# FFN down projection: nine of eleven feature pairs as 2x2x2 block products with their operands prepared in the gate/up stage and kept in DRAM

## The chip, the cores and the metric

The kernel runs on one core of a Trainium2 chip. The metric is the device time of one execution in microseconds. The kernel before takes 2179.9 us (median of three runs, 2179.11 to 2181.13).

## The reference

One step of a streaming encoder layer on 1056 rows (1024 new frames of one stream and 32 frames of another), width 1024: a half-step FFN, a token mixer (stick-breaking attention and gated linear attention beside each other), a second half-step FFN and a closing norm. The FFNs are where the change is:

```python
def swiglu(h, w_gate, w_up, w_down):
    return (jax.nn.silu(h @ w_gate) * (h @ w_up)) @ w_down

x = x + 0.5 * swiglu(rmsnorm(x, g_ffn1), w1g, w1u, w1d)
...
x = x + 0.5 * swiglu(rmsnorm(x, g_ffn2), w2g, w2u, w2d)
```

`w_gate` and `w_up` are 1024 x 2816, `w_down` is 2816 x 1024, all in float32. The 2816 hidden features are 22 tiles of 128, or eleven pairs of tiles.

## The kernel before, in words

Everything is kept transposed: features on the 128 partitions, the 1056 rows along the free dimension (`x[0..7]` are eight tiles of 128 x 1056). To keep float32 accuracy every operand is split into a high and a low part in the type fp32r: ACT copies the high part, DVE subtracts to get the low part (`split_to`, L51 and L55; POOL does the subtraction at L53 in some places). A product is then three matmuls: high by high, high by low, low by high (`mm3`, L60 to L62).

**Gate and up** are already computed as 2x2x2 block products with seven products in the place of eight (`Step`, `PRODUCTS`, `ORDER`). For each of ten feature pairs there are two steps, one for gate and one for up. A step takes the products in the order 1, 6, 7, 5, 2, 4, 3; each is 24 matmuls with 264 moving columns (L334): four k-tiles, two column slices, three split terms. The sums live in four PSUM tiles `acc_a` to `acc_d` of two banks. Products 1, 7 and 5 write a, c and d; products 2, 4 and 3 add to the same tiles later in the step, so that TensorE must wait until the first contents have been read: c1 by ACT (L347), u2, u3 and the outputs by DVE (L350, L353, L374, L380, L383). POOL makes the sums of weight blocks of the next step (L305 to L318) and, in an up step, three of the four multiplications gate by up (L384). The finished hidden tiles go to DRAM through the SP queue (`hid_spill`, L386). The first pair of each FFN is computed plainly (`Opening`).

**Down** (`Down.run`) is plain: the 22 hidden tiles come back from DRAM in groups of 4, 4, 4, 4, 2, 4, are split by ACT and DVE into `h[0..3]` and `h[4..7]` by turns, and for each of eight output tiles and three chunks of 352 columns the `mm3` of the group's tiles are summed in one PSUM tile `pd`; DVE adds half of it to `x` (L507). `Down.head` loads the first group while the last up step runs. In the last group the chunks are the outer loop, so that the norm of the next stage can start on a finished chunk.

The instructions of each engine stand in one queue and run in order. Their order is not the order in which the code emits them: a scheduler moves an instruction ahead or behind others of its engine where its operands and buffers allow. DMAs are issued from the SP queue, in its order.

Of the kernel before, what the change touches and what calls it, by code (L numbers as in the profile page):

```python
# [8 lines left out]
F32 = mybir.dt.float32  # L9
# [6 lines left out]
P = 128  # L16
# [13 lines left out]
def cs(c):  # L30
    return slice(c * CW, (c + 1) * CW)
# [93 lines left out]
}  # L125
ORDER = (1, 6, 7, 5, 2, 4, 3)


# [144 lines left out]
class Step:  # L273
# [89 lines left out]
    def out(self, q, u, ps):  # L363

        S, nc = self.S, self.S.nc
        two = lambda t: t.rearrange("p (s n) -> p s n", s=2)
        slot = lambda n: S.x[4 + q][:, n * HALF : n * HALF + HALF]
        if self.gate is None:
            sg = self.sg
            sg[q] = two(slot(1))  # L370
            if u is None:
                nc.scalar.activation(sg[q], ps, AF.Silu)
            else:
                nc.vector.tensor_add(sg[q], u, ps)  # L374
                nc.scalar.activation(sg[q], sg[q], AF.Silu)
        else:
            sg = self.gate.sg[q]
            hid = slot(0)
            if u is None:
                nc.vector.tensor_mul(two(hid), sg, ps)  # L380
            else:
                t = two(S.tmp.tile([P, HALF], F32, name="tc", tag="tc"))
                nc.vector.tensor_add(t, u, ps)  # L383
                nc.gpsimd.tensor_mul(two(hid), t, sg)  # L384
# [12 lines left out]
def gate_up(S, H, op, steps, among, between, tail, xd):  # L397
# [31 lines left out]
    for t in range(N):  # L429
        for p in ORDER:  # L430
# [4 lines left out]
            if p == 7 and t < N - 1:  # L435
                steps[t + 1].split_w()
            if t == 2 and p == 3:
                for d in range(4):
                    S.nc.sync.dma_start(S.x[d], xd[d])
            if t == N - 1:  # L440
                tail(p)

# [3 lines left out]

GROUPS = [4, 4, 4, 4, 2, 4]


class Down:  # L450


    def __init__(self, S, wd):
        self.S, self.src = S, wd
        self.n = 0

    def slab(self, raw, tag, pool):
        S = self.S
        r = raw()
        S.nc.sync.dma_start(r, self.src[self.n])  # L460
        self.n += 1
        w = pool.tile([P, 2, 1024], F32R, name="whl", tag=tag)
        split_to(S, w[:, 0], w[:, 1], r)
        return w

    def head(self, p):

        S, nc = self.S, self.S.nc
        if p in (6, 7, 5, 2):
            i = (6, 7, 5, 2).index(p)  # L470
            for h in range(2):
                raw = S.raw.tile([P, 1024], F32, name="wraw", tag="wraw")[:, :HALF]
                cols = slice(h * HALF, h * HALF + HALF)
                nc.sync.dma_start(raw, S.hidden[i][:, cols])
                split_to(S, S.h[i][:, 0, cols], S.h[i][:, 1, cols], raw)
        if p in (5, 4):
            raw2 = lambda: S.raw2.tile([P, 1024], F32, name="wraw2", tag="wraw2")
            self.first = getattr(self, "first", []) + [self.slab(raw2, "w", S.wp)]

    def run(self, after):  # L480
        S, nc = self.S, self.S.nc
        raw = lambda: S.raw.tile([P, 1024], F32, name="wraw", tag="wraw")
        f0 = 0
        for gi, n in enumerate(GROUPS):
            per = KT // n
            slabs = dict(enumerate(self.first)) if gi == 0 else {}
            base = 4 * (gi % 2)

            def get(j):
                if j not in slabs:  # L490
                    slabs[j] = self.slab(raw, "wd", S.wd)
                return slabs[j]

            def load(i):
                t = S.hraw.tile([P, NR], F32, name="hraw", tag="hraw")
                nc.sync.dma_start(t, S.hidden[f0 + n + i])
                h = S.h[4 - base + i]
                split_to(S, h[:, 0], h[:, 1], t)

            def one(d, c):  # L500
                w = get(d // per)
                pd = S.ps.tile([P, CW], F32, name="pd", tag="acc")
                for i in range(n):
                    o = i * (D // n) + (d % per) * P
                    mm3(nc, pd, w, slice(o, o + P), S.h[base + i], cs(c), i == 0, i == n - 1)
                xs = S.x[d][:, cs(c)]
                nc.vector.scalar_tensor_tensor(xs, pd, 0.5, xs, op0=ALU.mult, op1=ALU.add)  # L507

            if gi == len(GROUPS) - 1:
                for c in range(NCH):  # L510
                    for d in range(KT):
                        one(d, c)
                        if c and d == 1:
                            after(c - 1)
            else:
                m = GROUPS[gi + 1]
                for d in range(KT):
                    for c in range(NCH):
                        one(d, c)
                    if d * m // KT != (d + 1) * m // KT:  # L520
                        load(d * m // KT)
            f0 += n

# [687 lines left out]
def body(tc, A):  # L1211
# [10 lines left out]
    with ExitStack() as top:  # L1222
# [32 lines left out]
        S.wp = pool("wp", 2)  # L1255
        S.hidden = A["hid"]

        def up_pools(es, between=None):
            pool = opener(es)
            S.ps = pool("psf", 4, space=PSUM)  # L1260
            parts = pool("parts")
            S.X = [parts.tile([P, 2, HALF], F32R, name=f"part{k}") for k in range(12)]
            S.tmp = pool("tmp", 2)
# [4 lines left out]
        def down_pools(es):  # L1268
            pool = opener(es)
            S.wd, S.hraw, S.tmp = pool("wd", 4), pool("hraw", 2), pool("tmpd", 2)  # L1270
            S.ps = pool("psd", 8, space=PSUM)
# [16 lines left out]
        with ExitStack() as es:  # L1288
            up_pools(es)
            H = Halves(S, gains[:, 0], (1, 2, 3))  # L1290
# [36 lines left out]
            nc.vector.tensor_copy(S.maskb, consts[:, 2])  # L1327
        with ExitStack() as es:
            down_pools(es)
            for d in range(4, KT):  # L1330
                nc.sync.dma_start(S.x[d], A["x"][d])

# [6 lines left out]
            lr = gla_lowrank(S, A, G)  # L1339
            down.run(mix_norm)  # L1340
            q0, k0 = gla_qk(S, A, 0)
# [114 lines left out]
        with ExitStack() as es:  # L1456
# [46 lines left out]

            up_pools(es, outs)
            op.load(2)
# [17 lines left out]
            gate_up(S, H, op, steps, lambda j, n: [], between, down.head, xs)  # L1523
        with ExitStack() as es:
            down_pools(es)
            for d in range(4, KT):
                nc.sync.dma_start(S.x[d], xs[d])

# [9 lines left out]

            down.run(final)
            final(NCH - 1)  # L1540
# [20 lines left out]
def layouts(i):  # L1561
# [4 lines left out]
    def down(w):  # L1566
        out, f = [], 0
        for m in GROUPS:
            out.append(w[f * P : (f + m) * P].reshape(m, P, m, D // m).transpose(2, 1, 0, 3).reshape(m, P, D))
            f += m  # L1570
        return c(np.concatenate(out))

# [55 lines left out]
```

## Time and profile before

| what | value |
|---|---|
| time, median of three runs | 2179.9 us |
| the profiled execution: time, span | 2184.58 us, 2182.5 us |
| TensorE (PE) busy | 2110.6 us, 97% of the span, 15252 matmuls |
| VectorE (DVE) busy | 1241.2 us, 57% |
| ScalarE (ACT) busy | 809.8 us, 37% |
| GpSimd (POOL) busy | 468.9 us, 21% |
| DMA moved | 183.86 MB |
| down stage of the first FFN | from 492.7 to about 743 us |
| down stage of the second FFN | from about 1915 us to the end |

PE's busy time hides little: matmuls overlap and their ends are modelled, so that the distance between the starts of matmuls that follow each other is the time that one costs. An engine that is 57% busy over the span can be the bound in a stage of its own.

### The profile page before, as it was taken

How to read it: one execution, taken by the hardware profiler on the slowest of the kernel's cores; microseconds unless marked ns; L12 is line 12 of the kernel's file. 1: busy time of each engine (PE TensorE's matmuls, PEld its weight loads, DVE VectorE, ACT ScalarE, POOL GpSimd, SP SyncE). 2: the span in 40 equal slices, each digit the busy share in tenths (PEclk: the TensorE clock that was granted, in tenths of full speed). 3: DMA queues.
4: the chain of work that ended last, by engine and by line, in shares of the span. 5: the costliest groups of instructions: out<-in, count | busy, mean ns of one | idle time of the engine just before them, and what ended most of it. 6: DMA issues, size and time to landing. Idle time of an engine off the chain costs nothing.

```text
span 2182.5 us, 36732 instructions
## 1 busy us (share of the span) xinstructions
PE 2110.6 (97%) x15252; PEld 2042.2 (94%) x15252; DVE 1241.2 (57%) x1946; ACT 809.8 (37%) x1374; POOL 468.9 (21%) x385
## 2 busy tenths in 40 slices
PE   7999999999999989999999988899999999999998
PEld 6899999999999978888898987899999999999997
DVE  6844444455435766286766687687444444454456
ACT  6522322332112443335555565364223223321115
POOL 0133333320000221122122312101343343200000
PEclk9999999999999999999999999999999999999999
DMA  4222222226322300102203042232222222253212
GB/s 171 89 79 79 78 79 79 79 92 200 108 69 80 108 30 29 37 30 66 76 22 98 27 131 70 77 120 98 70 89 78 70 89 78 77 194 116 79 50 80
DMA packets 73351, 183.86 MB, mean 84 GB/s; under 512 B 8320, under 2 KB 29088, under 8 KB 73184
## 3 DMA queue, kind: packets, MB, share of 16 engines
q1 hardware_dynamic: 73184, 181.51, 25.5%
q8 instruction: 120, 1.97, 0.4%
q14 instruction: 47, 0.39, 0.1%
HBM read 131.21 MB, written 43.52 MB: 80 GB/s over the span
## 4 chain that ended last, share of the span: by engine, by line
PE 84%; DVE 10%; ACT 3%; issue 1%; DMA 1%; POOL 0%; DVEq 0%; SPq 0%; ACTq 0%; POOLq 0%
PE acc_a L334 11%; PE acc_c L334 11%; PE acc_d L334 11%; PE pd L60 7%; PE pd L62 7%; PE pd L61 7%; PE acc_b L334 5%; PE acc L242 4%; PE pj L60 3%; PE pj L61 3%; PE pj L62 3%; DVE f L1082 2%; PE st L587 2%; PE av L1107 1%; PE po L61 1%
## 5 line engine op out<-in xcount | busy, mean ns | idle before, releaser
L60 PE MATMUL pd<-h,whl 128*128 128x352 f32 x1056 | 342.6, 324 | 0.0
L62 PE MATMUL pd<-h,whl 128*128 128x352 f32 x1056 | 339.7, 322 | 0.0
L61 PE MATMUL pd<-h,whl 128*128 128x352 f32 x1056 | 339.7, 322 | 0.0
L334 PE MATMUL acc_a<-h,whl 128*128 128x264 f32 x1920 | 247.8, 285 | 2.0 <-DVE whl L55 2.0
L334 PE MATMUL acc_d<-part,S 128*128 128x264 f32 x1920 | 246.8, 284 | 0.0
L334 PEld LDWEIGHTS acc_a<-h,whl 128*128 128x128 f32 x1920 | 240.2, 189 | 2.2 <-DVE whl L55 2.2
L507 DVE SCALAR_TENSOR_TENSOR x<-pd,x 128x352 f32<-128x352 f32 x288 | 147.4, 521 | 162.9 <-PE pd L62 161.9
L334 PEld LDWEIGHTS acc_d<-part,S 128*128 128x128 f32 x1920 | 238.8, 188 | 0.0
L51 ACT ACTIVATE whl<-wraw 128x1024 fp32r<-128x1024 f32 x120 | 126.7, 1056 | 275.4 <-PE pd L62 190.0
L51 ACT ACTIVATE S<-s 128x512 fp32r<-128x512 f32 x160 | 101.3, 634 | 336.1 <-PE acc_d L334 155.4
L60 PE MATMUL pj<-h,whl 128*128 128x352 f32 x576 | 205.8, 357 | 0.0
L61 PEld LDWEIGHTS pd<-h,whl 128*128 128x128 f32 x1056 | 199.2, 189 | 0.4
L60 PEld LDWEIGHTS pd<-h,whl 128*128 128x128 f32 x1056 | 198.1, 188 | 0.4
L62 PEld LDWEIGHTS pd<-h,whl 128*128 128x128 f32 x1056 | 198.5, 188 | 0.0
L55 DVE TENSOR_TENSOR whl<-wraw,whl 128x1024 fp32r<-128x1024 f32 x92 | 137.2, 1492 | 100.0 <-ACT whl L51 100.0
L61 PE MATMUL pj<-h,whl 128*128 128x352 f32 x576 | 192.8, 335 | 0.0
L62 PE MATMUL pj<-h,whl 128*128 128x352 f32 x576 | 192.5, 334 | 0.0
L53 POOL TENSOR_TENSOR whl<-wraw,whl 128x1024 fp32r<-128x1024 f32 x28 | 70.6, 2522 | 371.0 <-ACT whl L51 370.9
L384 POOL TENSOR_TENSOR x<-tc,x 128x528 f32<-128x528 f32 x60 | 104.4, 1740 | 119.8 <-DVE tc L383 113.5
L334 PE MATMUL acc_b<-h,S 128*128 128x264 f32 x960 | 124.6, 285 | 1.5 <-ACT h L51 1.2
L334 PE MATMUL acc_c<-part,S 128*128 128x264 f32 x960 | 124.4, 285 | 1.1 <-DVE hid L254 1.1
L334 PE MATMUL acc_c<-h,A 128*128 128x264 f32 x960 | 123.6, 285 | 0.0
(285 smaller groups left out, 3813.5 us busy)
## 6 DMA issues: line engine op xcount, KB each, us to landing
hid_spill<-x SPq DMA_DIRECT2D x80, 264.0 KB, 2.1
hraw<-hid_spill SPq DMA_DIRECT2D x36, 528.0 KB, 4.6
wraw<-win SPq DMA_DIRECT2D x24, 512.0 KB, 3.3
wraw<-w1g SPq DMA_DIRECT2D x22, 512.0 KB, 3.7
wraw<-w1u SPq DMA_DIRECT2D x22, 512.0 KB, 3.3
wraw<-w1d SPq DMA_DIRECT2D x22, 512.0 KB, 3.8
wraw<-w2g SPq DMA_DIRECT2D x22, 512.0 KB, 3.5
wraw<-w2u SPq DMA_DIRECT2D x22, 512.0 KB, 3.3
```

Of the source, the lines that this page charges most:

```text
L51: nc.scalar.activation(hi, src, AF.Copy)
L53: nc.gpsimd.tensor_sub(lo, src, hi.bitcast(F32))
L55: nc.vector.tensor_sub(lo, src, hi.bitcast(F32))
L60: nc.tensor.matmul(out, w[:, 0, wsl], a[:, 0, asl], start=first, stop=False)
L61: nc.tensor.matmul(out, w[:, 0, wsl], a[:, 1, asl], start=False, stop=False)
L62: nc.tensor.matmul(out, w[:, 1, wsl], a[:, 0, asl], start=False, stop=last)
L242: nc.tensor.matmul(out, self.w[i](k, a), quarter(S, k, b, j), start=k == 0 and n == 0, stop=k == KT - 1 and n == 2)
L334: nc.tensor.matmul(t[:, s, :SW], w[:, a, ks], m(k, b, s), start=fresh and k == 0 and n == 0, stop=k == 3 and n == 2, skip_group_check=not ...
L384: nc.gpsimd.tensor_mul(two(hid), t, sg)
L507: nc.vector.scalar_tensor_tensor(xs, pd, 0.5, xs, op0=ALU.mult, op1=ALU.add)
L587: nc.tensor.matmul(st[:n, groups * b : groups * b + groups], sq[:, b * P : b * P + n], ones[:, :: P // groups], start=True, stop=True)
L1082: nc.vector.tensor_tensor_scan(fr, fr, fr, 1.0, op0=ALU.mult, op1=ALU.bypass)
```

## The change

Pairs 1 to 9 of each FFN (hidden tiles 2 to 19) take part in block products in the down projection too; pair 0 and pair 10 (tiles 0, 1, 20, 21) stay plain and come last.

In the gate/up stage the up step no longer stores hidden tiles for pairs 1 to 9. It keeps the seven moving operands of the pair: the blocks B11, B21, B22 and the differences T1 to T4, each split into high and low (ACT copy, DVE subtract) in one of `x[0..3]` by turns, and sends each (528 KB) to DRAM. B12 itself is not kept. The four differences are made by DVE when the last hidden block is there:

```diff
-            f, h = 2 * self.i + q // 2, q % 2
-            nc.sync.dma_start(S.hidden[f][:, h * HALF : h * HALF + HALF], hid)
+            if self.i == FT // 2 - 1:
+                f, h = 2 + q // 2, q % 2
+                nc.sync.dma_start(S.hidden[f][:, h * HALF : h * HALF + HALF], hid)
+            elif q != 1:
+                self.keep({0: "B11", 3: "B22", 2: "B21"}[q], hid)
+            else:
+                b11, b12, b21, b22 = (S.x[4 + n][:, :HALF] for n in range(4))
+                for name, o, x, y in (("T1", b11, b12, b11), ("T3", b12, b22, b12), ("T2", b22, b22, b11), ("T4", b21, b21, b22)):
+                    nc.vector.tensor_sub(o, x, y)
+                    self.keep(name, o)
+
+    def keep(self, name, src):
+        S = self.S
+        S.n_kept = getattr(S, "n_kept", 0) + 1
+        t = S.x[S.n_kept % 4].bitcast(F32R).rearrange("p (a n) -> p a n", a=2)
+        split_to(S, t[:, 0], t[:, 1], src)
+        S.nc.sync.dma_start(S.parts[self.i - 1, PARTS.index(name)], t.bitcast(F32))
```

The down stage is 20 steps: five groups of pairs, (1, 2), (3, 4), (5, 6), (7, 8) and (9), and in each group four steps, one for each pair of output tiles. A product of a group of two pairs is 12 matmuls of 264 columns, of the single pair 6. A step's weights are four blocks of the pair's weight tiles; POOL makes S1 to S4 of them, ACT and DVE split all seven:

```diff
+PAIRS = [(1, 2), (3, 4), (5, 6), (7, 8), (9,)]
+PLAIN = (0, 1, 20, 21)
...
+class DownStep:
...
+        nc.gpsimd.tensor_add(s1, a[3], a[2])
+        nc.gpsimd.tensor_sub(s2, s1, a[0])
+        nc.gpsimd.tensor_sub(s3, a[0], a[3])
+        nc.gpsimd.tensor_sub(s4, a[1], s2)
...
+        split_to(S, wa[:, 0, : 2 * w], wa[:, 1, : 2 * w], raw[:, : 2 * w])
+        split_to(S, ws[:, 0, : 2 * w], ws[:, 1, : 2 * w], s12)
+        split_to(S, wb[:, 0, :w], wb[:, 1, :w], a[2])
+        split_to(S, ws[:, 0, 2 * w : 4 * w], ws[:, 1, 2 * w : 4 * w], s34)
...
+        half = lambda out, ps, y: nc.vector.scalar_tensor_tensor(out, ps, 0.5, y, op0=ALU.mult, op1=ALU.add)
...
+            if p == 1:
+                c1 = new("s1")
+                nc.scalar.activation(c1, ps, AF.Copy, scale=0.5)
+            elif p == 6:
+                u2 = new("u2", bufs=1)
+                half(u2, ps, c1)
+            elif p == 7:
+                u3 = new("u3", bufs=1)
+                half(u3, ps, u2)
+                nc.gpsimd.tensor_add(x[1][1], x[1][1], u3)
+            elif p == 5:
+                half(x[1][1], ps, x[1][1])
+                nc.gpsimd.tensor_add(x[1][0], x[1][0], u2)
+            elif p == 2:
+                half(x[0][0], ps, x[0][0])
+                nc.gpsimd.tensor_add(x[0][1], x[0][1], u2)
+            elif p == 4:
+                half(x[1][0], ps, x[1][0])
+            else:
+                half(x[0][1], ps, x[0][1])
```

`w` is 256 for a group of two pairs and 128 for the single pair; s12 and s34 have one buffer each, `ws` (tag "w", called whl in the rows below) two. The parts of the next group are loaded from DRAM while a group runs, into the half of `h` and of the twelve tiles `X` that the group does not use. During the last four steps the four plain tiles are loaded and split (`plain_tile`), and four slabs of weights with them (`plain_slab`); `Down.plain` is then the last group of the kernel before. The weights of the down projection are laid out anew on the host.

What this does to the queues, at three places. **DVE in the down stage before**: between the additions to x (L507) stand only the splits of the next group's hidden tiles and slabs.

```order
L507 SCALAR_TENSOR_TENSOR x<-pd,x 128x352 x8
L55 TENSOR_TENSOR whl<-wraw,whl 128x1024
L507 SCALAR_TENSOR_TENSOR x<-pd,x 128x352 x5
L55 TENSOR_TENSOR h_84<-hraw,h_84 128x1056
L507 SCALAR_TENSOR_TENSOR x<-pd,x 128x352
L55 TENSOR_TENSOR h_85<-hraw,h_85 128x1056
```

DVE in a step of the down stage now (the 14th of the 20; u_7083 and u_7115 are its u2 and u3, S_7213, A_7214 and whl are the weights of the step two further on):

```order
L505 SCALAR_TENSOR_TENSOR u_7083<-pd_b,s_7065 128x528
L505 SCALAR_TENSOR_TENSOR u_7115<-pd_c,u_7083 128x528
L505 SCALAR_TENSOR_TENSOR x<-pd_d,x 128x528
L505 SCALAR_TENSOR_TENSOR x<-pd_a,x 128x528
L55 TENSOR_TENSOR S_7213<-wraw_7067,S_7213 128x512
L505 SCALAR_TENSOR_TENSOR x<-pd_c,x 128x528
L55 TENSOR_TENSOR A_7214<-wraw_7067,A_7214 128x256
L505 SCALAR_TENSOR_TENSOR x<-pd_d,x 128x528
L55 TENSOR_TENSOR whl<-s_7207,whl 128x512
L55 TENSOR_TENSOR whl<-s_7208,whl 128x512
```

The two splits that read the POOL sums s_7207 and s_7208 have moved to the end of the step, behind the last addition to x.

**POOL in the down stage**: before, three memsets are all that stands there between the last multiplications of the up step (L384) and the splits of the next stage (L53).

```order
L384 TENSOR_TENSOR x<-tc,x 128x528 x2
L573 MEMSET nv 128x9 x2
L1125 MEMSET fs 32x2
L384 TENSOR_TENSOR x<-tc,x 128x528
L53 TENSOR_TENSOR whl<-wraw,whl 128x1024 x2
```

Now (s_7085 are the sums for the 15th step, u_6961 and u_6993 are u2 and u3 of the 13th, s_7207 the sums for the 16th, u_7083 and u_7115 u2 and u3 of the 14th; L533 and L536 add u2 to two quarters of x, L530 adds u3 to the quarter that product 5 completes):

```order
L484 TENSOR_TENSOR s_7085<-wraw_6945 128x256
L485 TENSOR_TENSOR s_7085<-s_7085,wraw_6945 128x256
L486 TENSOR_TENSOR s_7086<-wraw_6945 128x256
L487 TENSOR_TENSOR s_7086<-wraw_6945,s_7085 128x256
L533 TENSOR_TENSOR x<-x,u_6961 128x528
L536 TENSOR_TENSOR x<-x,u_6961 128x528
L530 TENSOR_TENSOR x<-x,u_6993 128x528
L484 TENSOR_TENSOR s_7207<-wraw_7067 128x256
L485 TENSOR_TENSOR s_7207<-s_7207,wraw_7067 128x256
L486 TENSOR_TENSOR s_7208<-wraw_7067 128x256
L487 TENSOR_TENSOR s_7208<-wraw_7067,s_7207 128x256
L533 TENSOR_TENSOR x<-x,u_7083 128x528
```

The sums for step i+2 stand in front of the three additions of step i.

**DVE at the end of an up step** in the gate/up stage. Before, u2 and u3 of the next gate step follow the last output at once:

```order
L383 TENSOR_TENSOR tc<-u_4212,acc_d 128x528
L55 TENSOR_TENSOR S_4375<-s_4373,S_4375 128x512
L350 TENSOR_TENSOR u_4434<-s_4407,acc_b 128x528
L55 TENSOR_TENSOR S_4440<-s_4438,S_4440 128x512
L353 TENSOR_TENSOR u_4468<-u_4434,acc_c 128x528
```

Now (L394 are the differences T1 to T4, the splits named x<-x their low parts):

```order
L384 TENSOR_TENSOR tc<-u_4355,acc_d 128x528
L55 TENSOR_TENSOR S_4539<-s_4537,S_4539 128x512
L394 TENSOR_TENSOR x<-x 128x528 x2
L55 TENSOR_TENSOR x<-x 128x528
L394 TENSOR_TENSOR x<-x 128x528
L55 TENSOR_TENSOR x<-x 128x528
L394 TENSOR_TENSOR x<-x 128x528
L55 TENSOR_TENSOR x<-x 128x528 x2
L351 TENSOR_TENSOR u_4598<-s_4571,acc_b 128x528
L55 TENSOR_TENSOR S_4604<-s_4602,S_4604 128x512
L354 TENSOR_TENSOR u_4632<-u_4598,acc_c 128x528
```

Eight instructions have come between the last output of the up step and u2 of the next gate step.

More of the change, by code (lines that the diff above doesn't have):

```diff
@@ L480, in run @@
[L480 to L501, printed above, removed]
+        self.slab = 0
@@ new lines, in __init__, with part, load_part @@
+        h, X = S.h, S.X
+        h0 = lambda d: h[d][:, :, :HALF]
+        h1 = lambda d: h[d][:, :, HALF:]
+        self.places = [
+            [h0(0), h0(1), h0(2), h0(3), h1(0), h1(1), h1(2), h1(3)] + X[:6],
+            X[6:] + [h0(4), h0(5), h0(6), h0(7), h1(4), h1(5), h1(6), h1(7)],
+        ]
+        self.steps = [DownStep(self, g, m) for g in range(len(PAIRS)) for m in range(4)]
+        self.raw = {}
+    def part(self, g, n, k):
+        return self.places[g % 2][2 * n + k]
+    def load_part(self, g, n):
+        for k, i in enumerate(PAIRS[g]):
+            self.S.nc.sync.dma_start(self.part(g, n, k).bitcast(F32), self.S.parts[i - 1, n])
@@ new lines, in prep, with head, strassen, between @@
+    def prep(self, i):
+        if i < len(self.steps):
+            self.steps[i].prep(self.raw.pop(i))
+    def head(self, p):
+        if p == 1:
+            self.load_step(0)
+            self.load_step(1)
+        elif p == 6:
+            for n in range(4):
+                self.load_part(0, n)
+        elif p == 7:
+            self.load_part(0, 4)
+            self.load_part(0, 5)
+            self.prep(0)
+        elif p == 5:
+            self.load_part(0, 6)
+    def strassen(self, xd):
+        S = self.S
+        last = len(PAIRS) - 1
+        for d in range(4, KT):
+            S.nc.sync.dma_start(S.x[d], xd[d])
+        for i, st in enumerate(self.steps):
+            def between(n):
+                if n == 0:
+                    self.load_step(i + 2)
+                if n == 1:
+                    self.prep(i + 1)
+                if st.g < last and n % 2 == 0 and 4 * (n // 2) + st.m < 7:
+                    self.load_part(st.g + 1, 4 * (n // 2) + st.m)
+                if st.g == last and n in (1, 4):
+                    self.plain_tile(st.m, n // 4)
+                if st.g == last and n == 6:
+                    self.plain_slab(st.m)
+            st.emit(between)
@@ L522, in run @@
-            f0 += n
+                if c and d == 1:
+                    after(c - 1)
 def run(items, filler=()):
@@ L1255, in body, with ffn_pools @@
         S.wp = pool("wp", 2)
[L1256 to L1261, printed above, removed]
+        S.hidden, S.parts = A["hid"], A["parts"]
+        def ffn_pools(es, part, inner, between=None):
+            S.ps = opener(inner)("psf", 4, space=PSUM)
+            parts = opener(part)("parts")
             S.X = [parts.tile([P, 2, HALF], F32R, name=f"part{k}") for k in range(12)]
+            pool = opener(inner)
             S.tmp = pool("tmp", 2)
@@ L1327, in body @@
             nc.vector.tensor_copy(S.maskb, consts[:, 2])
[L1328 to L1331, printed above, removed]
+            down.strassen(A["x"])
+            inner.close()
+            plain_pools(es)
             def mix_norm(c):
@@ L1339, in body @@
             lr = gla_lowrank(S, A, G)
-            down.run(mix_norm)
+            down.plain(mix_norm)
             q0, k0 = gla_qk(S, A, 0)
@@ L1523, in body @@
             gate_up(S, H, op, steps, lambda j, n: [], between, down.head, xs)
[L1524 to L1527, printed above, removed]
+            down.strassen(xs)
+            inner.close()
+            plain_pools(es)
             def final(c):
@@ L1537, in final @@
                     nc.sync.dma_start(A["y"][d][:, cs(c)], t)
-            down.run(final)
+            down.plain(final)
             final(NCH - 1)
```

147 lines of the change are left out of this document (98 added, 49 removed).

## The prediction

> **What bounds the kernel now.** I read the page first, then the chain that ended last, then the busy time of single stretches.
>
> ```profile
> span 2182.5 us, 36732 instructions
> PE 2110.6 (97%) x15252; PEld 2042.2 (94%) x15252; DVE 1241.2 (57%) x1946; ACT 809.8 (37%) x1374; POOL 468.9 (21%) x385
> ...
> 115.94 2.93 PE acc_a L334 x24
> 118.86 2.92 PE acc_c L334 x24
> ...
> 385.00:440.00 55.00, 55.00 (x455) 55.00 (x454) 23.26 (x30) 17.30 (x26) 17.80 (x13) 1.00 0.21 69
> 550.00:605.00 55.00, 55.00 (x345) 55.00 (x344) 25.32 (x39) 9.43 (x9) 0.00 (x0) 1.00 0.32 98
> ```
>
> PE is the bound. In the gate/up stretch (385 to 440) and in the plain down stretch (550 to 605) it has no gap at the full clock, and the other engines are busy for less than half of the time; POOL does nothing in the down stretch. The chain gives the price of a product of the block form: 24 matmuls of 264 columns from 115.94 to 118.86, 2.92 us, 121.8 ns each. The down stretch gives the plain form: 345 matmuls of 352 columns touch 55.00 us, so 344 intervals, 159.9 ns each. So the first question is how many matmuls go, and the second whether the other engines, which had half of their time free, can feed a stage whose products are half as long as those of gate and up.
>
> **The matmuls.** For one pair and one of four pairs of output tiles the plain form needs 2 x 2 x 3 x 3 = 36 matmuls of 352, 36 x 0.1599 = 5.76 us; the block form 7 x 2 x 3 = 42 matmuls of 264, 42 x 0.1218 = 5.12 us. That is 0.64 us less, 9 pairs x 4 x 2 FFNs = 72 times: **-46 us** if PE never waits. The Trainium skill (TensorE: Matmul & The Clock Gate, "Back-to-back issue gap") gives for streams with weight loads about 81 ns at 128 columns and 131 ns at 512; between them by a straight line, an estimate, 352 columns would cost 110 ns and 264 columns 99 ns, and the block form would be the slower one by 13 us in all. The two rows above contradict it here: the shorter matmul is 38 ns cheaper.
>
> **The queues of a down step with two pairs.** PE needs 7 x 1.46 = 10.24 us. These rows price the rest, from the groups and from the timeline:
>
> ```profile
> L507 DVE SCALAR_TENSOR_TENSOR x<-pd,x 128x352 f32<-128x352 f32 x288 | 147.4, 521 | 162.9 <-PE pd L62 161.9 <-issue 0.8
> L350 DVE TENSOR_TENSOR u<-s,acc_b 128x528 f32<-128x528 f32 x40 | 28.2, 704 | 162.7 <-PE acc_b L334 162.7
> L55 DVE TENSOR_TENSOR S<-s,S 128x512 fp32r<-128x512 f32 x160 | 111.3, 697 | 4.5 <-ACT S L51 2.8
> L55 DVE TENSOR_TENSOR wt<-tr,wt 128x256 fp32r<-128x256 f32 x16 | 6.7, 417 | 4.2 <-ACT wt L51 4.2
> L55 DVE TENSOR_TENSOR h<-wraw,h 128x528 fp32r<-128x528 f32 x16 | 11.4, 711 | 12.8 <-ACT h L51 12.7
> L305 POOL TENSOR_TENSOR s<-wraw 128x512 f32<-128x512 f32 x38 | 48.9, 1288 | 210.1 <-DVE S L55 210.1
> ...
> 443.95 0.69 DVE L55 TENSOR_TENSOR S<-s,S 128x512 fp32r<-128x512 f32 x1
> 444.01 1.84 POOL L384 TENSOR_TENSOR x<-tc,x 128x528 f32<-128x528 f32 x1 [0.91 <-DVE tc L383]
> 445.81 1.29 POOL L305 TENSOR_TENSOR s<-wraw 128x512 f32<-128x512 f32 x1
> 446.15 0.70 DVE L380 TENSOR_TENSOR x<-x,acc_a 128x528 f32<-128x528 f32 x1 [1.51 <-PE acc_a L334]
> 447.18 1.29 POOL L308 TENSOR_TENSOR s<-s,wraw 128x512 f32<-128x512 f32 x1
> 447.25 2.30 DVE L55 TENSOR_TENSOR whl<-wraw,whl 128x1024 fp32r<-128x1024 f32 x1 [0.39 <-ACT whl L51]
> 468.20 1.23 DVE L55 TENSOR_TENSOR whl<-wraw,whl 128x1024 fp32r<-128x1024 f32 x1 [3.17 <-ACT whl L51]
> 484.97 1.32 POOL L384 TENSOR_TENSOR x<-tc,x 128x528 f32<-128x528 f32 x1 [21.41 <-DVE tc L383]
> ```
>
> The timeline rows show first that a DVE split and a POOL operation exclude each other: POOL at 444.01 takes 1.84 us instead of the 1.32 us that it takes alone at 484.97, since a split began just before it; the split at 447.25 takes 2.30 us instead of the 1.23 us at 468.20, since POOL began before it. A DVE operation that reads PSUM (446.15, 0.70 us) is not held by POOL, nor holds it.
>
> Prices: an L505 operation of 528 columns reads one PSUM operand like L350 (704 ns) and is the form of L507 (521 ns for 352): 0.70 us. A split of 512 is 0.69, of 256 0.42. POOL's additions to x are the 528-column form, 1.32 us alone. POOL's sums of 256 columns no row shows: half of the 1.29 us of 512 columns is 0.65, and with a fixed part (1.32 at 528 against 1.29 at 512 is 1.9 ns a column) it would be 0.80; I take 0.67, near the half.
>
> Now the order. The addition L505 that completes product 5's quarter (first x<-pd_d of a step) waits for POOL's L530, and product 3 adds to pd_d and so waits for that L505. POOL's queue has in front of it L533 and L536, and in front of these the four sums for the step two ahead. These have one buffer each, so they wait for the two whl splits at the end of DVE's previous step, and those stand in DVE's queue behind everything from the previous step's first x<-pd_d on. That is a ring: DVE from the first x<-pd_d to the last whl split, 4 x 0.70 + 0.69 + 0.42 + 2 x 0.69 = 5.29 us; then POOL, 4 x 0.67 + 3 x 1.32 = 6.64 us; then DVE again. 11.93 us, and about 0.3 us for some fifteen handovers of 0.02 to 0.07 us (443.95 + 0.69 to 444.01 and the like): **12.25 us a step against PE's 10.24, so PE waits 2.0 us at product 3 of each step.** The sums can't slip under the last split, because of the exclusion; without that the ring would be 0.7 shorter. With sums of 0.80 it would be 0.5 longer. So 1.3 to 2.5 us.
>
> The ring is not closed in the first steps, where the sums were made ahead, and is looser in the last two, whose sums are of 128 columns: of 16 steps I count 12.5. 12.5 x 2.0 = 25 us for each FFN, **+50 us** (33 to 63). This also lengthens the time that loads have.
>
> **The four steps of the single pair.** PE needs 7 x 0.73 = 5.12 us each, 20.5 us in all, yet every reading of PSUM is as long as before. By the queue, DVE has from the first of these steps on 24 L505 (16.8 us), six splits of 528 columns (0.71, 4.3 us), four of 512 (2.8), six of 256 (2.5) and two of 128 (0.28 by the step from 697 to 417 ns, 0.6): 27.0 us. POOL has 12 x 1.32 and eight sums of 128 columns (a quarter of 1.29 and a bit, 0.36): 18.7 us. Each step is again a chain: product 6, u2 (0.70), three POOL additions (4.0), the addition to pd_d's quarter (0.70), product 3 and the next step's products 1 and 6 (2.2) and 0.4 of handovers make 8.0 us, and the splits between (2.5 us a step) and the sums (0.7) stand in POOL's way: 11.2. Four such steps are 45 us, which is also the two engines' sum (45.7): 25 us lost in each FFN, **+50 us**. If only the splits excluded POOL, 10.2 + 18.7 = 28.9 us would do and 8.4 would be lost: 17 to 55 us.
>
> **The gate/up stage.** For each of 18 pairs it gains 7 ACT copies, 7 splits (0.71) and 4 differences (0.70, as L350): 7.8 us more of DVE in the 40.9 us of two steps, where the row from 385 to 440 has 23.26 / 55 x 40.9 = 17.3 us. So there is room on average. What counts is the stretch behind the up step's last product: output, POOL's multiplication and a split (2.7 us), four differences and four splits (5.6 us) with the copies of ACT between, and only then u2, a split and u3 of the gate step (2.1 us). From the product's end at 20.7 us after the step's start DVE comes to u3's end at about 33.5 if it was free then, and at 35.9 if it was 2.4 us behind, from splits earlier in the step that waited for POOL's multiplication and then for its turn. u3 must have read acc_c when product 4 of the gate step starts, 12 products x 2.92 = 35.1 us. So 0 to 0.8 us a pair; I take 0.3: **+5 us** (0 to 15). SP's queue holds the loads of weight tiles behind the seven writes; the last write goes out some 11 us into the gate step, and the weights loaded behind it are first summed two steps later, so I cost that at nothing.
>
> **The parts' way through DRAM.**
>
> ```profile
> hraw<-hid_spill SPq DMA_DIRECT2D x36, 528.0 KB, 4.6
> ...
> 495.00:500.00 5.00, 5.00 (x33) 5.00 (x32) 0.92 (x2) 0.00 (x0) 1.16 (x1) 1.00 0.95 350
> ```
>
> A group of two pairs loads 14 x 528 KB and 4 x 512 KB, 9.7 MB, while the group before runs: 198 GB/s over 4 x 12.25 us, against 350 GB/s that the row at 495 shows in five microseconds. The first group's parts are issued product by product as the last up step releases their places; 7.6 MB at 350 GB/s take 22 us, and the last of them is needed some 26 us after the first can start. I take 0; at 200 GB/s the head would be about 8 us late in each FFN.
>
> **Sum.** -46 + 50 + 50 + 5 = +59, with 1 us for the two handovers of PSUM to the plain group +60. Against the profiled execution (2184.58 us, span 2182.5) that is 2244.6; it ran 0.2% above the median of the runs, so against the median, 2179.9, it is **2240 us**. About 0.2%, 4.4 us, can be told from no change here.
>
> **The rivals.** *PE stays fed* (0.09): the ring closes in PE's time. It decides at 10.24 us, so it has to be 2.0 us shorter, as when POOL's additions took 0.65 us in the place of 1.32. Then only the single pair's lower bound remains, -46 + 17: 2151 us. For it: the stage was free on three engines, and the orders come from a scheduler. Against it: 1.32 us is what POOL takes alone, and the order puts the sums in front of the additions.
> *The rings are looser* (0.14): DVE and POOL overlap more than the rows allow, waits of 1.4 us in a step and steps of 9 us in the single pair: -46 + 35 + 31 + 5 = +25, 2205 us; with every lower bound (-46 + 33 + 17) it is 2184.
> *The parts come late* (0.06): at 170 GB/s a group needs 57 us in the place of 49; 8 us for each of three groups and the head in each FFN are 64 us more, 2304 us.
> *As worked out* (0.69): 2240 us, 2215 to 2262 with one term at a time at its bounds. 0.02 are left for causes that I don't see.
>
> **The numbers.** The range, 2196 to 2263, leaves out the fed PE, the late parts and the lowest end of the looser rings, about 0.2. Faster by over 0.2%: 0.09 and a little of the looser rings, 0.1. Within 0.2%: 0.04, the looser rings at their lower bounds. Slower: 0.86.
>
> **What would show it.** In the profile after, gaps of PE in front of pd_d matmuls with DVE as the releaser, about 2 us, once in each step of the groups of two pairs; steps of 12.25 us in the chain; POOL busy from the sums to L530 without a gap and then idle; steps of about 11 us in the single pair; gate/up steps still at 2.92 us a product. I am wrong if the steps take 10.24 us; if PE waits for DMA (the parts) or for weights; or if gate and up lose more than 1 us a pair.

## The result, and the profile after

| | before | after |
|---|---|---|
| time, median of four runs each | 2180.52 us (2179.11 to 2184.93) | 2207.61 us (2206.37 to 2211.17) |
| ratio, with 95% interval | | 1.0123 [1.0105, 1.0142] |
| the profiled execution: time, span | 2184.58 us, 2182.5 us | 2208.22 us, 2206.4 us |
| down stage of the first FFN, first matmul to the start of the last | 492.7 to 750.0 us | 492.0 to 760.3 us |

The down stage before ends at about 750 us, and not at 743 as in the first table. The change makes the kernel 27 us slower; 60 were forecast. The direction and the place are the forecast's, the size isn't: the value lies at the lower end of the range. Where 27 us in the place of 60 come from is the subject of what follows. One of the ten executions of experiment 5 below ran at a granted clock of 0.84 and took 2278.64 us; its time there is the median of the other nine.

The page after, its span, the engines' busy time and the group of the addition that completes pd_d's quarters (the last two columns are the idle time of DVE ahead of it and what ended it):

```profile
span 2206.4 us, 38879 instructions
PE 2089.5 (95%) x15684; PEld 2011.2 (91%) x15684; DVE 1441.0 (65%) x2240; ACT 908.6 (41%) x1636; POOL 764.2 (35%) x665
...
L505 DVE SCALAR_TENSOR_TENSOR x<-pd_d,x 128x528 f32<-128x528 f32 x80 | 56.5, 706 | 131.1 <-POOL x L530 127.5
```

PE is busy for 21 us less than before, in a span that is 24 us longer. It now waits, and DVE, which lets it go on, has itself stood idle for 131.1 us in front of this one group, 127.5 us of them for POOL's L530, the addition of u3. The longest of PE's waits after (what it waited for, then the total, times and longest):

```profile
PE pd_d L516 <- DVE x L505: 36.7, 33, 2.8
```

This is the wait that was forecast, at product 3. It has the forecast's place, but only 36.7 us. The three stretches of the first FFN's down stage after: the first steps with two pairs, the four steps of the single pair, and the first 11 us of the plain group behind them (busy time and count of PE, PEld, DVE, ACT, POOL; then the granted clock, the DMA share and GB/s):

```profile
492.00:655.90 163.90, 154.17 (x1244) 151.81 (x1243) 87.82 (x144) 40.44 (x72) 103.37 (x103) 1.00 0.65 242
...
669.10:709.00 39.90, 27.10 (x170) 24.58 (x169) 29.62 (x48) 11.89 (x25) 21.17 (x23) 0.88 0.29 91
709.00:720.00 11.00, 11.00 (x59) 11.00 (x58) 7.70 (x12) 3.25 (x6) 2.40 (x1) 0.81 0.45 150
```

And the same place of the plain group before, 70 matmuls in 11 us at the full clock, where after has 59 at 0.81:

```profile
700.00:711.00 11.00, 11.00 (x70) 11.00 (x69) 6.77 (x10) 3.44 (x6) 2.41 (x1) 1.00 0.46 138
```

The account for each FFN, from the starts of matmuls (the first FFN's numbers): the 16 steps with two pairs run from 492.01 to 669.09, 177.1 us, where 16 x 10.24 = 163.8 would do: 13.2 lost. The single pair's four steps run to 709.04, 39.95 us against 20.5: 19.5 lost. The plain group takes 51.2 us from its first matmul's start to its last one's, 49.2 before: 2.0 lost, and 2.9 in the second FFN (50.2 against 47.3). PE's own gain is the 208.1 us that before takes for its first 1296 down matmuls less 184.2 of block products: 23.9. So 13.2 + 19.5 + 2.0 - 23.9 = +10.8 in the first FFN, and 11.7 with the second one's plain group; the rest of the 24 us of span, 1.5 us, lies outside the down stages.

**One closed step.** DVE and POOL after, from one first x<-pd_d to the next, put together in the order of time from the timeline (start, duration; in brackets the idle time before and what ended it):

```profile
566.01 0.71 DVE L505 SCALAR_TENSOR_TENSOR x<-pd_d,x 128x528 f32<-128x528 f32 x1 [3.73 <-POOL x L530]
566.63 0.69 DVE L505 SCALAR_TENSOR_TENSOR x<-pd_a,x 128x528 f32<-128x528 f32 x1
567.25 0.68 DVE L55 TENSOR_TENSOR S<-wraw,S 128x512 fp32r<-128x512 f32 x1
567.85 0.70 DVE L505 SCALAR_TENSOR_TENSOR x<-pd_c,x 128x528 f32<-128x528 f32 x1
568.46 0.41 DVE L55 TENSOR_TENSOR S<-wraw,S 128x256 fp32r<-128x256 f32 x1
568.79 0.70 DVE L505 SCALAR_TENSOR_TENSOR x<-pd_d,x 128x528 f32<-128x528 f32 x1
569.41 1.28 DVE L55 TENSOR_TENSOR whl<-s,whl 128x512 fp32r<-128x512 f32 x2
570.23 1.07 POOL L484 TENSOR_TENSOR s<-wraw 128x256 f32<-128x256 f32 x1 [4.25 <-issue]
571.38 0.73 POOL L485 TENSOR_TENSOR s<-s,wraw 128x256 f32<-128x256 f32 x1
...
576.01 1.33 POOL L530 TENSOR_TENSOR x<-x,u 128x528 f32<-128x528 f32 x1
577.38 0.71 DVE L505 SCALAR_TENSOR_TENSOR x<-pd_d,x 128x528 f32<-128x528 f32 x1 [3.73 <-POOL x L530]
```

This is the ring of the prediction, member by member. POOL has no gap from L484 to L530, and L484 is held by the last split, 1.07 us where the next sum has 0.73. Its length is 577.38 - 566.01 = 11.37 us, not 12.25. POOL's part, from the last split's end at 570.69 to L530's end at 577.34, is 6.65 us (forecast 6.64). DVE's part is 4.68 us, from 566.01 to 570.69; the forecast had 5.29, and 0.3 for handovers, of which the rows show 0.04 (577.34 to 577.38). Look at the starts: 566.01, 566.63, 567.25. Each operation is listed with about 0.70 us, and yet the next starts 0.62 us behind it. The durations overlap. Added up, they charge DVE for time that it doesn't spend, some 0.08 us each.

### The profile page after: what moved, and what is told of

Its sections match the earlier page's. It is cut to its first block, busy times and chain, and to the rows that moved or that the text cites. A ratio compares the mean times of both kernels' runs of the same rounds, so it can differ in the third digit from the quotient of the medians.

```text
span 2206.4 us, 38879 instructions
## 1 busy us (share of the span) xinstructions
PE 2089.5 (95%) x15684; PEld 2011.2 (91%) x15684; DVE 1441.0 (65%) x2240; ACT 908.6 (41%) x1636; POOL 764.2 (35%) x665
## 5 line engine op out<-in xcount | busy, mean ns | idle before, releaser
L51 ACT ACTIVATE x<-x 128x528 fp32r<-128x528 f32 x126 | 81.4, 646 | 203.9 <-DVE x L394 95.3
L319 POOL TENSOR_TENSOR s<-wraw,s 128x512 f32<-128x512 f32 x38 | 49.1, 1293 | 281.7 <-DVE S L55 281.7
L55 DVE TENSOR_TENSOR x<-x 128x528 fp32r<-128x528 f32 x126 | 96.0, 762 | 71.1 <-ACT x L51 68.5
L505 DVE SCALAR_TENSOR_TENSOR x<-pd_d,x 128x528 f32<-128x528 f32 x80 | 56.5, 706 | 131.1 <-POOL x L530 127.5
L53 POOL TENSOR_TENSOR whl<-wraw,whl 128x1024 fp32r<-128x1024 f32 x28 | 69.6, 2486 | 170.9 <-ACT whl L51 170.7
L55 DVE TENSOR_TENSOR S<-s,S 128x512 fp32r<-128x512 f32 x160 | 123.5, 773 | 3.8 <-ACT S L51 2.5
L335 PEld LDWEIGHTS acc_b<-h,S 128*128 128x128 f32 x960 | 120.2, 188 | 1.9 <-ACT h L51 1.4
L335 PEld LDWEIGHTS acc_c<-part,S 128*128 128x128 f32 x960 | 119.6, 188 | 1.3 <-DVE hid L255 1.3
L335 PEld LDWEIGHTS acc_c<-h,A 128*128 128x128 f32 x960 | 119.7, 189 | 0.0
L306 POOL TENSOR_TENSOR s<-wraw 128x512 f32<-128x512 f32 x38 | 48.9, 1288 | 198.1 <-DVE S L55 198.1
```

The source lines that it names most:

```text
L51: nc.scalar.activation(hi, src, AF.Copy)
L53: nc.gpsimd.tensor_sub(lo, src, hi.bitcast(F32))
L55: nc.vector.tensor_sub(lo, src, hi.bitcast(F32))
L306: eng.tensor_add(self.s1, a21, a22)
L319: eng.tensor_sub(src, a12, self.s2)
L335: nc.tensor.matmul(t[:, s, :SW], w[:, a, ks], m(k, b, s), start=fresh and k == 0 and n == 0, stop=k == 3 and n == 2, skip_group_check=not ...
```

## The experiments

The theory (T1): the ring holds the steps with two pairs; the single pair's steps are held by DVE and POOL; nothing else costs. The rivals: DVE's readings of PSUM as a whole set the step, or the parts from DRAM do.

**1. The addition of u3 behind product 5's half.** It cuts the ring: DVE's first x<-pd_d no longer waits for POOL, and the sum x + u3 + p/2 is made in the other order.

```diff
                 half(u3, ps, u2)
-                nc.gpsimd.tensor_add(x[1][1], x[1][1], u3)
             elif p == 5:
                 half(x[1][1], ps, x[1][1])
+                nc.gpsimd.tensor_add(x[1][1], x[1][1], u3)
```

> One edit to the changed kernel: GpSimd's addition of u3 to x[1][1] moves from behind product 7 to behind product 5's half, so DVE's first x<-pd_d of a step waits for no GpSimd work. Theory 1 (the ring of DVE's queue, GpSimd's sums, GpSimd's additions and DVE again holds back product 3 in the steps with two pairs): the ring is cut, these steps fall from 11.37 us to PE's 10.24, the 13.2 us that a block stage loses in its first 16 steps go, and the time falls by about 26 us to 2181 us (2173 to 2186); the four steps of the single pair change little. Rival A (DVE as a whole, the reading of PSUM, sets the step): no change, 2207 us. Rival B (the parts from DRAM set it): no change, 2207 us.

Measured: 2161.14 us, 0.9916 [0.9900, 0.9933] of before; 46 us less than the changed kernel, where 26 were expected. The same three stretches in this kernel:

```profile
493.00:656.70 163.70, 163.70 (x1347) 163.70 (x1346) 109.25 (x161) 45.63 (x83) 111.40 (x110) 1.00 0.67 247
656.70:689.00 32.30, 24.15 (x170) 22.38 (x168) 31.77 (x47) 12.32 (x26) 20.92 (x20) 0.95 0.33 104
689.00:700.00 11.00, 10.96 (x68) 10.96 (x69) 8.30 (x13) 3.11 (x7) 3.29 (x5) 1.00 0.50 169
```

PE has no gap in 163.7 us: the 16 steps run at 10.23 us each, with the same DVE and POOL work beside them. So T1 holds there, and DVE as a whole isn't the bound. What was not expected is the rest: the single pair's four steps take 32.4 us in the place of 39.95, and the plain matmuls behind them have the full clock, 68 in 11 us. In the single pair's steps DVE is now busy for 31.77 of 32.30 us, its splits lengthened by POOL (up to 1.56 us for 256 columns, against 0.42): it seems to be the bound here, which no run tests by itself. Experiments 5 and 6 take the two effects apart.

**2. The four weight sums on DVE.** `nc.gpsimd.tensor_add(s1, ...)` and the three below it become `nc.vector`.

> One edit to the changed kernel: the four weight sums of a down step are made by DVE and not by GpSimd. Theory 1 (the ring): GpSimd keeps 3.9 us of 6.65 in the ring, DVE gets four operations of about 0.33 us (a split of 256 has about 0.33 start to start), 8.5 us of DVE in a step against PE's 10.24: the steps with two pairs run at 10.24 us, the time falls by about 26 us to 2181 us, a little more if the single pair's steps gain too. Rival A (DVE as a whole sets the step): 1.3 us more of DVE in each of 12 steps of each FFN, +31 us, 2238 us. Rival B (the parts from DRAM): no change, 2207 us.

Measured: 2191.49 us, 1.0044 [1.0029, 1.0059] of before: 16 us less than the changed kernel, not 26, and no sign of the 31 us more of the DVE rival. The steps with two pairs take 10.42 us. DVE in one of them:

```profile
564.52 0.71 DVE L505 SCALAR_TENSOR_TENSOR x<-pd_d,x 128x528 f32<-128x528 f32 x1 [2.80 <-POOL x L530]
...
569.80 0.42 DVE L485 TENSOR_TENSOR s<-s,wraw 128x256 f32<-128x256 f32 x1
570.13 0.70 DVE L505 SCALAR_TENSOR_TENSOR u<-pd_b,s 128x528 f32<-128x528 f32 x1
...
574.93 0.71 DVE L505 SCALAR_TENSOR_TENSOR x<-pd_d,x 128x528 f32<-128x528 f32 x1 [2.78 <-POOL x L530]
```

The ring is not gone, it has another composition: three of the sums stand in front of u2 in DVE's queue, POOL's three additions wait for u2, and DVE waits for the last of them again. 564.52 to 574.93 is 10.41 us, 0.17 more than PE needs, and PE follows. The expectation had counted the engines' work and not the new ring. In this kernel the single pair is as slow as ever (40.5 us in the first FFN, 39.3 in the second), and the plain group begins at a clock of 0.85.

**3. No loads of the later groups' parts.** `if st.g < last and ...: self.load_part(...)` is switched off, so 98 of the 126 loads stay away (the expectation's 118 is a miscount), and the later groups are multiplied with old parts.

> The changed kernel without the loads of the parts for the second and later groups of pairs in the down stage (118 of 126 loads of 528 KB stay away; the products then use the first groups' parts, so the output is not the reference's). Theory 1 (the ring): the steps with two pairs stay at 11.37 us and those of the single pair at about 10; no change, 2207 us (2202 to 2209). Rival B (the parts come late, or the DMA traffic slows the engines' accesses): the losses of the 16 steps go, about 2181 us.

Measured: 2210.70 us, 1.0138 [1.0123, 1.0153] of before: nothing gained. The DMA rival is out. A side result explains a detail. Here the steps 3 and 4 take 11.37 us, and in the changed kernel 10.22. POOL after in step 3, and then POOL of this kernel in the same step:

```profile
520.15 1.32 POOL L530 TENSOR_TENSOR x<-x,u 128x528 f32<-128x528 f32 x1
521.43 0.74 POOL L484 TENSOR_TENSOR s<-wraw 128x256 f32<-128x256 f32 x1
```

```profile
518.03 0.74 POOL L487 TENSOR_TENSOR s<-wraw,s 128x256 f32<-128x256 f32 x1
518.73 1.33 POOL L533 TENSOR_TENSOR x<-x,u 128x528 f32<-128x528 f32 x1
```

With the loads in the program the scheduler put the sums behind the additions in these two steps, and the ring is open there. So four of the changed kernel's 16 steps are free (1, 3, 4 and 15), one is half so, and some 11 carry the full 1.13 us: the 12.5 of the forecast were near.

**4. The ninth pair plain too.** Four groups of two pairs, then six plain tiles in two phases (2 tiles, 4 tiles); the first four plain tiles and three slabs are loaded and split in the last group of two.

```diff
-PAIRS = [(1, 2), (3, 4), (5, 6), (7, 8), (9,)]
+PAIRS = [(1, 2), (3, 4), (5, 6), (7, 8)]
```

> The changed kernel with the ninth pair plain as well: eight pairs in four groups of two as block products, the last three pairs plain (first the ninth pair's two tiles, then the four of the last two pairs). Theory 1 (DVE and GpSimd bound the single pair's steps): its 39.95 us become 144 matmuls of 352 columns at 0.160, 23.0 us, 16.9 us less in each FFN; and the plain matmuls behind it, which then follow work without gaps, run at the full clock and not at 0.81 and 0.72 (2.4 us in each FFN): -38 us, 2169 us (2164 to 2176). If the lower clock behind the single pair has another cause than PE's gaps there: -34 us, 2174 us. Rival (the single pair's steps are slow because the end of the block part must drain DVE and GpSimd anyway): the wait only moves to the last group of two, and no more than half is won, 2188 us or more.

Measured: 2177.65 us, 0.9986 [0.9977, 0.9995] of before: 30 us less than the changed kernel, between the two expectations (2169 and 2188). Only 23 us of the 30 come from the two down stages, which take 512.1 us together against 535.3; in its profile the mixer between the FFNs, which the edit does not touch, was 12 us shorter (see the last section). So the stages lie nearer to the rival's 19 than to the 38 of the theory. The plain work is as expected, 72.7 us for 432 matmuls at the full clock. But the block part takes 184.3 us where the 16 steps took 177.1. PE in the last group:

```profile
642.84 1.63 PE L516 MATMUL pd_b<-part,whl 128*128 128x264 f32 x12
...
652.41 2.70 PE L516 MATMUL pd_d<-h,whl 128*128 128x264 f32 x12 [2.09 <-DVE x L505]
654.91 2.23 PE L516 MATMUL pd_a<-part,S 128*128 128x264 f32 x12
656.97 1.62 PE L516 MATMUL pd_b<-part,whl 128*128 128x264 f32 x12
```

From one product 6 to the next 14.13 us: the splits of the plain tiles and slabs stand in the ring. They make DVE's part 1.9 us longer, and POOL's sums beside them, held up by further splits, 0.9 us. And behind a gap of 2.09 us twelve matmuls take 2.50 us (652.41 to 654.91) and not 1.46.

**5 and 6. Experiment 1 in halves.** u3's addition late in the groups of two alone, and in the single pair alone (`if self.n == 2` and `if self.n == 1` ahead of it, the early place for the other).

> The later addition of u3 in the sixteen steps with two pairs alone; the four steps of the single pair as in the changed kernel. If the ring and the single pair's steps are two separate losses: the steps with two pairs run at 10.24 us (13.2 us less in each FFN), the single pair's four steps stay at 40 us, with PE waiting 2 to 3 us at pd_d, and the first matmuls behind them still run at half the clock: 2207.6 - 26.4 = 2181 us (2178 to 2185). If the single pair's steps were faster in the first experiment only because DVE came to them without a backlog: 2161 to 2168 us.

> The later addition of u3 in the four steps of the single pair alone. If the two losses are separate: the steps with two pairs stay at 11.37 us, the single pair's four take 32.4 us as in the first experiment (7.5 us less in each FFN), PE's gaps there stay under 2.5 us and the plain matmuls behind them keep the full clock (2.2 us less): 2207.6 - 19.4 = 2188 us (2184 to 2192). If the clock behind the single pair drops for another cause than PE's gaps: 2192 us or more, with the plain matmuls still at 290 ns at first. If the single pair's steps depend on the backlog from the steps before: 2200 us or more.

Measured: 2175.37 us, 0.9975 [0.9961, 0.9988] of before, which is 2.6 us below the expected range, and 2195.25 us, 1.0066 [1.0051, 1.0081]. By stages in the first FFN:

| | 16 steps of two pairs | four steps of the single pair | plain group |
|---|---|---|---|
| after | 177.1 us | 39.95 us | 51.2 us |
| 5, late in the pairs | 163.7 us | 37.6 us | 50.9 us |
| 6, late in the single pair | 177.0 us | 33.6 us | 49.5 us |
| 1, late in both | 163.7 us | 32.4 us | 49.5 us |

The losses are separate, but for 1 to 2 us that the single pair gains when DVE comes without a backlog. The single pair had a ring through u3 too, worth 6 us. PE at the end of the single pair in experiment 5, then in 6:

```profile
693.71 1.69 PE L516 MATMUL pd_d<-part,whl 128*128 128x264 f32 x6 [2.80 <-DVE x L505]
695.20 0.49 PE L60 MATMUL pd<-h,part 128*128 128x352 f32 x1
```

```profile
700.89 0.89 PE L516 MATMUL pd_d<-part,whl 128*128 128x264 f32 x6
703.06 0.43 PE L60 MATMUL pd<-h,part 128*128 128x352 f32 x1 [1.28 <-DVE x L505]
703.33 0.32 PE L61 MATMUL pd<-h,part 128*128 128x352 f32 x1
703.49 0.32 PE L62 MATMUL pd<-h,part 128*128 128x352 f32 x1
```

Behind a gap of 2.80 us matmuls of 264 columns come every 0.22 us (after a first one of 0.39) and those of 352 every 0.29; behind gaps of 1.42 and 1.28 us they come every 0.12 and 0.16. So the lower clock behind the single pair goes with PE's gaps (the last section has the rest). Experiment 6 is 3 us above its upper bound: its down stages gain 18.7 us together, nearly as expected, but the stretch between the two down stages, whose code the edit doesn't touch, took 1172 us in its profile against 1167 in the changed kernel's.

**7. Experiments 1 and 4 together.**

> Both edits that were worth most: u3's addition behind product 5's half, and the ninth pair plain. Block part of 16 steps at 10.24 us, 163.8 us, then 144 + 288 plain matmuls in 72 us. Against the first experiment (2161 us) the single pair's 32.4 us become 23 us in each FFN: 2143 us if DVE's splits for the plain pairs, which now lie in the last group's steps, find room there; but these 2.8 us of splits exclude GpSimd, 2.2 + 2.8 of splits and 6.65 of GpSimd make 11.65 us in the last three or four steps against PE's 10.24, 4 us more in each FFN: 2151 us. Range 2142 to 2155; the rival, that the wait only moves to the last group as in the fourth experiment (7 us there in each FFN), gives 2157 us.

Measured: 2145.09 us, 0.9840 [0.9825, 0.9854] of before: 38 us less than the kernel before in the same comparison (2182.94). The two stretches of the first FFN's down stage:

```profile
492.50:660.20 167.70, 164.86 (x1346) 164.01 (x1345) 117.14 (x168) 49.68 (x90) 111.33 (x105) 1.00 0.63 229
660.20:732.80 72.60, 70.86 (x437) 70.15 (x436) 53.06 (x103) 27.85 (x51) 12.94 (x10) 1.00 0.32 109
```

167.7 us, 3.9 above 163.8: the last two steps before the end take 11.8 and 12.7 us, since splits and POOL exclude each other, 4 us as worked out. The second FFN's block part takes 168.4. That the time is 2145 and not 2151 is again the stretch between the two down stages (1158 us here, 1167 in experiment 1). In the down stages alone experiment 7 gains 8 us on experiment 1, and 33 us on the kernel before.

**8. The disputed price.** The two whl splits of a step with two pairs made twice, to add two known operations to DVE's part of the ring.

```diff
         split_to(S, ws[:, 0, 2 * w : 4 * w], ws[:, 1, 2 * w : 4 * w], s34)
+        if self.n == 2:
+            nc.vector.tensor_sub(ws[:, 1, :512], s12, ws[:, 0, :512].bitcast(F32))
+            nc.vector.tensor_sub(ws[:, 1, 512:], s34, ws[:, 0, 512:].bitcast(F32))
```

> The changed kernel with the two whl splits of a step with two pairs each made twice by DVE (same data again), in the place where they stand. It lengthens DVE's part of the ring by two operations of 512 columns; the four steps of the single pair are as before. If a step is the ring, and DVE's part is to be priced from start to start (0.60 us each, as 569.41 - 568.79 and the like): closed steps of 11.37 + 1.20 = 12.57 us. By the durations as the profile lists them (0.69 us): 12.75 us. If these splits lie beside POOL's work and not in the ring: steps of 11.37 us. In the time, with 11 to 14 such steps in each FFN: 2207.6 + 26 to 34, about 2237 us.

One execution: 2242.78 us against 2180.6 of before. DVE's first x<-pd_d of two steps that follow each other, and PE behind the second (the edit adds three lines, so that L505, L516 and L530 are L508, L519 and L533 here):

```profile
600.05 0.71 DVE L508 SCALAR_TENSOR_TENSOR x<-pd_d,x 128x528 f32<-128x528 f32 x1 [3.64 <-PE pd_c L519]
...
612.60 0.71 DVE L508 SCALAR_TENSOR_TENSOR x<-pd_d,x 128x528 f32<-128x528 f32 x1 [4.92 <-POOL x L533]
```

```profile
613.37 3.01 PE L519 MATMUL pd_d<-part,whl 128*128 128x264 f32 x12 [2.05 <-DVE x L508]
616.17 1.83 PE L519 MATMUL pd_a<-h,S 128*128 128x264 f32 x12
```

12.55 us, as start to start prices it (12.57), not 12.75; thirteen of the 32 steps with two pairs take 12.5 to 12.6 us. The ring has the length that was read, and the operations in it cost their distance. The time is 6 us above the estimate, and the last rows show where it goes: the gap at product 3 has reached 2.05 us, and here the twelve matmuls behind it take 2.80 us in the place of 1.46. The four longest steps take 13.4 to 13.8 us.

## Why the prediction was wrong in size

- **The matmuls, -46: right.** 23.9 us for each FFN, -47.8. In experiment 1, 16 steps of 84 matmuls take 163.7 us, 121.8 ns each, the forecast's row. The estimate from the Trainium skill (TensorE: Matmul & The Clock Gate, "Back-to-back issue gap"), by which block products would have lost 13 us, doesn't hold here.
- **The ring, +50: the mechanism right, the size half.** This is the step that failed: "DVE from the first x<-pd_d to the last whl split, 4 x 0.70 + 0.69 + 0.42 + 2 x 0.69 = 5.29 us", with "about 0.3 us for some fifteen handovers". These are durations as listed; DVE's part is 4.68 us, and the handovers come to 0.04 us. The row that was to show them was misread: the split at 443.95 ends at 444.64, behind the POOL operation's start at 444.01, and hands nothing over. 11.37 us a step and not 12.25, so PE loses 1.13 us and not 2.0, which is also below the forecast's bounds of 1.3 to 2.5. What is left of each step is the difference of two large numbers, and an error of 7% in the ring is one of 43% in the loss: 13.2 us for each FFN and not 25. The trace of before had the right price:

```profile
449.47 0.69 DVE L383 TENSOR_TENSOR tc<-u,acc_c 128x528 f32<-128x528 f32 x1
450.09 0.68 DVE L55 TENSOR_TENSOR A<-wraw,A 128x512 fp32r<-128x512 f32 x1
```

  0.62 us from start to start beside 0.69 us listed. The Trainium skill says as much (Perfetto Trace Analysis, "Optimizing Scalar/DVE Operations"): the listed latency of a DVE operation holds its write acknowledgement, which overlaps with the next instruction. It puts the listed access overhead at about twice the engine's; the runs here show 0.08 us of overlap in 0.70.
- **The single pair, +50: too much as well, and incomplete.** It lost 19.5 us for each FFN and not 25: from one product 3 to the next PE takes 11.8, 10.3, 8.7 and 8.9 us, where 11.2 were forecast for each. The forecast took "the two engines' sum (45.7)", as if DVE and POOL never worked at the same time. They do: the window row has 29.62 + 21.17 = 50.8 us of listed work in 39.9 us, though a part of it is one holding the other up. About 6 of the 19.5 us were the ring through u3 (experiment 6); the rest is probably DVE's own work, which fills 98% of the stretch when that ring is cut (experiment 1).
- **Gate and up, +5: nothing.** The second FFN's gate/up steps, from their first block product to the first down matmul, take 409.1 us before and after. Four rows of the passage from an up step to the next gate step, after:

```profile
410.20 3.07 PE L335 MATMUL acc_a<-h,whl 128*128 128x264 f32 x24
412.65 0.70 DVE L384 TENSOR_TENSOR tc<-u,acc_d 128x528 f32<-128x528 f32 x1
422.82 0.70 DVE L354 TENSOR_TENSOR u<-u,acc_c 128x528 f32<-128x528 f32 x1
424.81 0.41 PE L335 MATMUL acc_c<-h,A 128*128 128x264 f32 x2
```

  The backlog came about: PE is done with the up step at 410.2 us, and DVE turns to its output 2.4 us later. Even so u3 (422.82) ends 1.29 us before product 4 starts at 424.81; before, it was 4.93 us. The forecast's terms, 20.7 + 2.7 + 5.6 + 2.1, make 31.1 us behind the step's start, and 33.5 with the backlog; the trace has 33.8. The 35.9 us that gave the +5 counts the backlog twice.
- **The parts through DRAM, 0: right** (experiment 3).
- **Not foreseen: PE's clock.** Waits of about 2 us and more can halve the rate of matmuls for 3.4 us or twice that (last section): 2.0 and 2.9 us lost in the two plain groups behind the single pair, and part of the loss inside it.

Put together with what was measured, the forecast's sum is 2 x (-23.9 + 13.2 + 19.5 + 2.4) + 1 = +23, against +24 of span. "The rings are looser" came out in its number (2205 us, chance 0.14) but in the ring not for its reason, which was that DVE and POOL overlap more: in a closed step they exclude each other as forecast, and it is DVE's operations that overlap with each other. In the single pair DVE and POOL did overlap more than the sum of 45.7 us allows. The range "2215 to 2262 with one term at a time at its bounds" doesn't follow from the bounds given, which make 2207 to 2253; that the measured time meets the lower edge is chance, since there a single term was to be at its bound, and in the runs all three were smaller, the ring with 26 us even below its bound of 33.

## What to carry to other kernels

The time of a busy queue, in these traces, is the sum of the distances between starts, not of the durations that a profile lists; where a forecast is the difference of two nearly equal times, this decides it. When a step is held by a ring of two engines, look for the one member that can change its place before counting anyone's work: an addition moved by one product turned +27 us into -20, and moving work to the other engine instead only made another ring. A stage whose products become half as long while its reads of PSUM stay as long (the single pair here) was better left in the plain form: 23 us for 144 matmuls against 31 to 40 in block form, of which the splits that then move into the last group took 4 to 5 us back (experiment 7).

## What the runs showed of the hardware

**The clock of the matmuls goes by windows of 3.41 us.** Where the single pair of the changed kernel ends, matmuls of 352 columns start every 0.29 us up to about 713 us, and every 0.16 us from then on:

```profile
709.04 0.50 PE L60 MATMUL pd<-h,part 128*128 128x352 f32 x1
...
713.30 0.32 PE L60 MATMUL pd<-h,part 128*128 128x352 f32 x1
```

The mean clock of 0.81 in the row from 709 to 720 hides half the rate for 4 us. In the ten traces the granted clock changes only at times that lie whole multiples of 3.41 us apart, and it is 1.00 or 0.50. The changed kernel, cut at these times (columns as above: busy time and count of PE, PEld, DVE, ACT and POOL, then the granted clock, the DMA share and GB/s):

```profile
685.81:689.22 3.41, 1.61 (x14) 1.40 (x12) 0.85 (x2) 0.31 (x1) 3.20 (x5) 1.00 0.28 79
689.22:692.63 3.41, 2.75 (x21) 2.62 (x21) 3.41 (x5) 1.26 (x3) 1.49 (x2) 1.00 0.01 2
692.63:696.05 3.42, 1.87 (x12) 1.35 (x11) 3.42 (x7) 0.61 (x1) 1.29 (x1) 1.00 0.18 25
696.05:699.46 3.41, 3.41 (x15) 3.41 (x16) 2.48 (x4) 0.00 (x0) 1.32 (x1) 0.50 0.53 208
...
702.87:706.29 3.42, 1.00 (x6) 0.78 (x6) 1.44 (x3) 0.00 (x0) 3.42 (x3) 1.00 0.47 161
706.29:709.70 3.41, 2.15 (x9) 2.15 (x10) 2.36 (x4) 0.42 (x1) 0.57 (x4) 0.50 0.26 63
```

What counts is how long PE idles within one window (3.41 us less its listed busy time), and not how long a gap is. In the down stages of the nine profiles with block products, every window at the full clock in which PE idled for 1.9 us or more was followed by one at half clock (33 windows), and none with less than 1.55 us was; in between, 5 were (with 1.55 us the one from 692.63) and 16 were not (with 1.80 us the one from 685.81), and what decides there stays open. Most gaps that seem to contradict each other are explained by it. The 2.46 us in front of 689.88 are cut by the border at 689.22 and slow nothing; 0.70 and 0.94 us in front of 691.25 and 693.20 in experiment 6 lie in one window and, together, bring half the rate. In experiment 8 a gap of 2.05 us in front of 613.37 lies within one window and halves the rate, and one of 2.05 us in front of 515.09 is cut by a border and doesn't. The Trainium skill (TensorE: Matmul & The Clock Gate, Part 1 and "Why this matters for your kernels") has half rate after an idle window of about 3.4 us, and advises against gaps of more than about 3 us. The half rate and the 3.4 us agree; but here a window need not be idle throughout, and gaps of 2 us were enough.

**The stretch between the two down stages** took 1155 to 1172 us in these nine profiles. The second FFN's gate/up part of it took 409.1 us in each. What moves is the mixer, from the last plain matmul of the first FFN to the first gate/up matmul of the second: 698.7 us in experiment 4, 702.0 in experiment 7, and 708 to 716 in the others. No edit is in its code, and in all nine each engine runs the same instructions there in the same order. PE's idle time hardly differs (38.6 us in experiment 4, 41.1 in experiment 6 with 715.7 us), but PE is busy for 660 us in the one and 675 us in the other, at a granted clock of 0.97 and 0.95. So the spread goes with the clock; why the clock differs was not tried. It is why the experiments are read by the stages here, and the totals only to within some 8 us.
